# Turning the PSUM banks from block to block, a w_ple product one row block later, and g_final in eight pieces

## The chip, the cores and the metric

The kernel runs on one core of a Trainium2 chip. The metric is the device time of one execution, in microseconds (us), as the median over several runs. The engines are TensorE (PE in the profile, with its weight loads as PEld), VectorE (DVE), ScalarE (ACT), GpSimd (POOL) and SyncE (SP). SP and POOL issue the DMAs.

## The reference

One encoder layer on 256 tokens of width 4096, in float32. Two groups of attention heads (latent attention and dilated window attention) come first; then the output projection, a gated embedding and a last norm. The change touches only what follows the output projection:

```python
x = x + concat([y_a, y_b]) @ w_out                      # (256, 4096)
ple  = p @ w_ple                                        # (256, 256) @ (256, 4096)
gate = sigmoid(rms_norm(x, g_ple) @ w_ple_gate)         # (256, 4096) @ (4096, 4096)
x = x + ple * gate
out = rms_norm(x, g_final)
```

## The kernel before

**A product in three parts.** Every float32 operand of a large product is split in two: `hi` is a copy rounded to a format that PE takes at full speed, made by ACT, and `lo` is the rest, made by DVE (`split`, line 244). `mm` (line 262) then issues three matmuls: hi x hi, hi x lo and lo x hi. Weights come from HBM by DMA into one of four `raw` buffers of 128 x 1024 floats, are split into a pair of tiles, and are used once. A raw buffer is free when DVE has made `lo`, and only then can SP issue the load that uses it next. The pair goes to a ring of three `wp` pairs and, in some stages, a few further buffers.

**Blocks and steps.** The layer is a list of steps, built once and run in order by the loop at the end of `encoder_layer`. A product of 256 x 4096 by 4096 x 1024 is a `Block` (line 1114). A plain step ("c") takes 128 rows of the weights: four products of 128 x 512 (two token tiles by two column halves), 12 matmuls in all. A part of the rows goes through Strassen's scheme of seven products ("f", four steps for each pair of row blocks). The eight sums of a block live in the eight PSUM banks, which have the names m0 to m3, s, o, t0 and t1. `LAST` (line 1504) gives the banks of the three blocks of `w_ple_gate`, in the order M2, X, M3, M4, M1, M5, M6, M7. M2, X, M3 and M4 are open from the first step of a block to its last; M1, M5, M6 and M7 are written by the fast steps only.

**The order in a block.** `spread` (line 1509) lays out six plain steps, 28 fast ones with eight plain ones between them, and four plain ones. For `w_ple_gate` it also puts an "e" into the last four: the product p @ w_ple for the same 1024 columns (`wide_ple`, line 1331), two steps of 12 matmuls, in the banks of M1, M5, M6 and M7. Two tasks empty the banks: `wide_mid` (line 1362) after the last fast step (one ACT copy out of M1, then four DVE additions out of M6, M5, M7 and M5 into the tile `e`, which is `B` in the profile), and `wide_done` (line 1374) after the block's last step (four DVE additions out of M2, X, M3 and M4, then tanh, the product with ple, the addition to x and the squares). After the w_ple product, ACT copies two of its four banks to `Q` and `junk`; the two in t0 and t1 are read in place by `wide_done`.

**Who goes first.** There is no scheduler at run time: each engine has one queue and runs it in the order in which the program was written. The writing is planned. A model of the engines' clocks gives each task a time from which it may go on (`advance`, line 423), and a task is only taken further when `room()` says that splitting the weights has time in hand. `convert_one` (line 1844) writes the splits some steps ahead of their use. So an addition that empties a bank can stand on DVE behind the split of a weight which PE needs only three steps later.

**The end.** Three blocks cover 3072 columns. The other 1024 are done without the fast scheme: two chunks of 512 columns and then 256 and 256 (numbers 6, 7 and 8 in `blocks`), with 32 row blocks each, taken two or four at a time. `tail_banks` (line 1709) names their banks. `g_final` is loaded as a row that is repeated over 128 partitions, in two DMAs of 128 x 2048 on POOL's queue (`load_g`, line 1324), into two buffers (`Al0` and `B5`) that the third block's fast steps read until late; a hook two steps into the tail writes them. `late_gains` (line 1461) multiplies the six finished column chunks by g_final, twelve DVE instructions spread over the tail's steps. `finish` (line 1468) scales each row and stores it.

Nearly all instructions are recorded by one helper, so that they have line 176 in the profile; its groups are told apart by their tiles.

Of the kernel before, what the change touches and what calls it, by code (L numbers as in the profile page):

```python
# [18 lines left out]
P = 128  # L19
# [190 lines left out]
def encoder_layer(ctx: ExitStack, tc: tile.TileContext, x, p, positions, g_mix, w_in, g_q_latent, w_uq,  # L210
# [15 lines left out]
    def slot(tag, shape, dtype=F32):  # L226
        names[tag] = names.get(tag, 0) + 1
        return clock.made(sp.tile([P, *shape], dtype, tag=tag, name=f"{tag}_{names[tag]}"), tag)
# [167 lines left out]
        yield max(flags.at[n] for n in names)  # L396

    begun, due = [-20.0], {}
    lazy = set()
    SOON = 0.3  # L400

    def spawn(task, later=False):
        urgent.append(task)
        due[task] = 0.0
        if later:
            lazy.add(task)

    def resume(pool, task):
        while True:
            clock.stage = 0.0  # L410
            got = next(task, "end")
            due[task] = max(clock.stage, due.get(task, 0.0), got if isinstance(got, float) else 0.0)
            if isinstance(got, Late):
                due[task] += 0.45 if "x dead" in flags else 0.3
            if got == "end":
                pool.remove(task)
                due.pop(task, None)
                lazy.discard(task)
                return
            if not isinstance(got, float) or due[task] > clock.free["pe"] + SOON:  # L420
                return

    def advance(force=False, spare=True):
        if force:
            ahead = [due.get(t, 0.0) for pool in (urgent, running) for t in pool]
            now = clock.free["pe"]
            clock.free["pe"] = max(now, min([d for d in ahead if d > now], default=now))
        now = clock.free["pe"]
        if waiting and len(running) < 5 and now - begun[0] >= waiting[0][2] and waiting[0][0] <= flags:
            needs, task, _ = waiting.pop(0)  # L430
            running.append(task)
            due[task] = max([flags.at[f] for f in needs], default=0.0)
            begun[0] = now
        for pool in (urgent, running):
            for task in list(pool):
                if due.get(task, 0.0) <= clock.free["pe"] + SOON and (force or (spare or task not in lazy) and room() > ROOM):
                    resume(pool, task)


# [659 lines left out]
    class Step:  # L1099
# [5 lines left out]

        def __init__(self, load, split, run, needs=(), frees=0, time=2.73):
            self.load, self.split, self.run, self.needs, self.frees, self.after = load, split, run, needs, frees, None
            self.hold = 0
            self.time = time
            self.ring, self.ring_id = WP, None  # L1110

# [209 lines left out]
        return add_sums(FAST, lambda j: [q[:, 2 * (j % 2):2 * (j % 2) + 2] for q in x1T[j // 2]], z_dst, "B3",  # L1321
                        "x1_sums", x1_s)

    def load_g(i):
        gF.append(slot(("Al0", "B5")[i], [2048]))
        nc.gpsimd.dma_start(gF[i], g_final[2048 * i:2048 * (i + 1)].unsqueeze(0).to_broadcast([P, 2048]))

    P4 = {}
    WIDE_PLE = {(0, 0): "m2", (0, 1): "m3", (1, 0): "t0", (1, 1): "t1"}

    def wide_ple(k):

        ps = {}

        def step(kt):
            box = []

            def load():
                box.append(clock.made(wp.tile([P, 2, Q], F32, tag="raw", name=f"raw_e{kt}", bufs=RAW), "raw", RAW))
                nc.sync.dma_start(box[0].rearrange("p a b -> p (a b)"),  # L1340
                                  w_ple[kt * P:(kt + 1) * P, 1024 * k:1024 * (k + 1)])

            def run(hi, lo):
                for (t, h), tag in WIDE_PLE.items():
                    if kt == 0:
                        ps[t, h] = bank(tag, [Q])
                    mm(ps[t, h], tuple(pT[0][:, i, kt, t * P:(t + 1) * P] for i in range(2)), (hi[:, h], lo[:, h]),
                       kt == 0, kt == 1)
                if kt:
                    spawn(out())  # L1350

            return Step(load, lambda hi, lo: split(hi, lo, box[0]), run, ["pT", ("mid", k)], 1)

        def out():
            for h in range(2):
                nc.scalar.activation(P4[0, h], ps[0, h], AF.Copy)
                P4[1, h] = ps[1, h]
            yield

        return [step(0), step(1)]  # L1360
# [63 lines left out]
    def g_cols(lo, n):  # L1424
        return gF[lo // 2048][:, lo % 2048:lo % 2048 + n]
# [32 lines left out]
                yield from finish(ts[0])  # L1458
        return task

    def late_gains():
        for c in range(2 * WIDE):
            for t in range(NT):
                nc.vector.tensor_tensor(x1[c][:, t], x1[c][:, t], g_cols(512 * c, 512), op=ALU.mult)
                yield
                yield

    def finish(t):
        r, a, h, w = r2[:, t:t + 1], stat(1), stat(1), stat(1)
# [31 lines left out]
        return w[:, lo:lo + n]  # L1501

    hooks = {}
    LAST = "m0", "m1", "s", "o", "m2", "m3", "t0", "t1"

    FAST_COST, PLAIN_COST, PLAIN_TIME = (1.8, 2.3, 1.15, 1.15), 1.15, 2.73
    FAST_TIME = 0.69, 1.37, 1.37, 1.37
# [20 lines left out]
    def lay(blk, order, mid, done, ple=None):  # L1528
        last = max(i for i, o in enumerate(order) if o == "f")
        n = order.count("f") // 4  # L1530
        fast = (x for j in range(n) for x in blk.fast_steps(j))
        rest = list(range(2 * n, 16)) + list(range(16, 32))
        if blk.late:
            rest = rest[16 - 2 * n:] + rest[:16 - 2 * n]
        plain_ = (x for kt in rest for x in blk.plain_step(kt))
        for i, kind in enumerate(order):
            new = {"f": lambda: [next(fast)], "c": lambda: [next(plain_)], "e": lambda: ple}[kind]()
            if i == last:
                new[-1].after = mid
            if i == len(order) - 1:  # L1540
                new[-1].after = done
            for x in new:
                x.ring, x.ring_id = blk.ring, blk
            steps.extend(new)
        return len(steps) - len(order) + last
# [150 lines left out]
                     lambda j: ["pT", ("wide", WIDE - 1)])  # L1696

    for k in range(WIDE):
        order = spread(FAST, 6, 4, (-2,))
        blk = Block(w_ple_gate[:, 1024 * k:1024 * (k + 1)], lhs_x1, x1_s, "x1_sums", order,  # L1700
                    lambda kt: [("x1T", kt // 4)], LAST, "Ah2", WP + ["Al2", "B0"])
        for tag in ("Al2", "B0"):
            allow(blk, tag, lambda i: ran[0] >= out_end - 1)
        blk.fast_needs = [("x1T", c) for c in range(8)]
        blk.turn_needs = [("wide", k - 1)] if k else []
        lay(blk, order, wide_mid(k, blk), wide_done(k, blk), wide_ple(k))
    wide_end = len(steps)
    hook(wide_end + 2, lambda: (load_g(0), load_g(1), spawn(late_gains(), True)))
    tail_banks = {6: (("m2", "m3"), ("t0", "t1")), 7: (("m0", "o"), ("s", "m1")), 8: (("m2", "m3"), ("t0", "t1"))}

    for c, (lo, n) in enumerate(blocks):
        if c < 2 * WIDE:
# [34 lines left out]
    class Old(Step):  # L1747


        def __init__(self, i, ch, j):  # L1750
            self.i, self.ch, self.j, self.ring, self.ring_id = i, ch, j, ch.ring, ch.ring_id
            self.needs, self.after, self.hold = ch.needs(j), None, 0
            self.time = ch.per * len(ch.ts) * 3 * (ch.n / 2370 + 0.011)
            kept_before = ch.keep and not ch.keep[1]
            self.banks = [ch.banks[t] for t in ch.ts] if j == 0 else ()
            self.load = None if kept_before else self.fetch
            self.frees = 0 if kept_before else 1
            self.own = kept_before or ch.keep and j < len(kept)
# [143 lines left out]
    for i, step in enumerate(steps):  # L1902
        if i in hooks:
            for f in hooks[i]:
                f()
        if i < 16 and i % 2 == 0 and 3 + i // 2 < 8:
            next(loads[3 + i // 2])
        lead = i + AHEAD + (3 if len(step.ring) > 3 else max(0, min(3, i - (len(steps) - 25))))
        fetch(lead + 3)
        if i < START:  # L1910
            if 0 < i < 16:
                x_bank((i + 8) % 16)
            if i == 2:
                x_square(8)
            convert(lead + 1)
        n = 0
        while not all(f in flags for f in step.needs) or any(b in locks for b in step.banks) or i not in halves:
            advance(True)
            convert(lead + 1)
            n += 1  # L1920
            assert n < 200, (i, step.needs)
        step_end[0] = clock.free["pe"] + step.time
        step.run(*halves.pop(i))
        ran[0] = i
        if step.after:
            spawn(step.after())
            advance()
        while slack(i) < MARGIN and convert_one(lead + 1):
            pass
        advance(spare=slack(i) > MARGIN)  # L1930
        convert(lead + 1)
# [23 lines left out]
```

## Time and profile before

| | |
|---|---|
| median of 3 runs | 1915.16 us (1914.77 to 1916.81) |
| the profiled execution | 1916.41 us |
| its span in the profile | 1914.6 us |
| PE busy | 1892.6 us, 99% of the span |
| DVE busy | 1636.3 us, 85% |
| ACT busy | 1115.9 us, 58% |
| DMA | 370.61 MB, mean 194 GB/s |

A row of the timeline gives the start in us from the span's start, the duration, the engine, the line, the operation with the tile it writes and those it reads, its shape and how often it was repeated. The brackets at its end hold the idle time of the engine just before it and what ended that time. A row of the chain that ended last gives start, duration and the piece of work, a row of the waits the engine that waited, for whom, the total in us, the number of times and the longest. A row of the DMA issues gives the tiles, the queue, the count, the size of one, and the median time in us from issue to landing, here for the stretch named in the text. Start times are rounded, and the ends of matmuls overlap the next one's start. From one matmul of 512 columns to the next it is 0.2267 us where nothing waits.

### The profile page before, as it was taken

Reading aid. Unit: us, or ns where it says so; the run is one execution under the profiler, and the core shown is the slowest. Engines: PE = TensorE matmul, PEld = TensorE weight load, DVE = VectorE, ACT = ScalarE, POOL = GpSimd, SP = SyncE. Lnnn points to the kernel's source line nnn. Section 1 sums busy time; section 2 is a strip of 40 time slices with the busy share of each in tenths; the row PEclk is TensorE's granted clock in tenths of the full one; section 3 lists DMA queues with packets and bytes.
Section 4 is the critical chain, followed back from the end, with each engine's and each line's share of the span. In section 5 each row is a group of like instructions: output and inputs, shape, how many; then the busy total and the mean of one; then the engine's idle time right before and its main releaser. Section 6 shows DMA issues by size and latency. Waiting matters only on the chain.

```text
span 1914.6 us, 25920 instructions
## 1 busy us (share of the span) xinstructions
PE 1892.6 (99%) x9451; PEld 1614.7 (84%) x9451; DVE 1636.3 (85%) x2276; ACT 1115.9 (58%) x1520; POOL 35.4 (2%) x50
## 2 busy tenths in 40 slices
PE   9999999999999999999999999999999999999997
PEld 6888888888899988888888999888888887888787
DVE  6999999898877789899998777798887988989865
ACT  7655556565577755556565555665554655665543
POOL 1000000000000100000000011000000000000000
PEclk9999999999999999999999999999999999999999
DMA  7566666666654466666667444566666556566665
GB/s 273 183 207 214 215 214 200 196 212 193 186 149 140 142 198 193 192 209 194 214 198 210 136 122 139 170 218 222 206 208 213 171 198 225 181 220 206 203 196 176
DMA packets 159792, 370.61 MB, mean 194 GB/s; under 512 B 28548, under 2 KB 70640, under 8 KB 159408
## 3 DMA queue, kind: packets, MB, share of 16 engines
q1 hardware_dynamic: 158640, 364.97, 60.1%
q0 software_dynamic: 1024, 3.99, 0.6%
q8 instruction: 74, 1.21, 0.3%
q14 instruction: 54, 0.44, 0.1%
HBM read 364.72 MB, written 4.19 MB: 193 GB/s over the span
## 4 chain that ended last, share of the span: by engine, by line
PE 82%; DVE 11%; DMA 3%; issue 2%; ACT 2%; SPq 0%; ACTq 0%; DVEq 0%
PE m L176 48%; PE t L176 15%; PE s L176 10%; PE o L176 9%; DVE lo L176 3%; DVE B L176 3%; DVE T L176 2%; DMA raw<-in_w_ple_gate_dram 2%; DVE Ah L176 1%; DMA raw<-in_w_in_dram 1%; DVE Al L176 1%; ACT hi L176 1%; DVE st L176 0%; ACT T L176 0%; ACT B L176 0%
## 5 line engine op out<-in xcount | busy, mean ns | idle before, releaser
L176 ACT ACTIVATE hi<-raw 128x1024 fp32r<-128x1024 f32 (+3 forms) x455 | 440.9, 977 | 353.7 <-PE t L176 87.1
L176 DVE TENSOR_TENSOR lo<-raw,hi 128x1024 fp32r<-128x1024 f32 (+3 forms) x455 | 505.3, 1120 | 117.2 <-ACT hi L176 114.0
L176 PE MATMUL m<-hi,Ah 128*128 128x512 f32 (+3 forms) x836 | 308.5, 381 | 2.3 <-ACT hi L176 1.8
L176 PE MATMUL m<-hi,Al 128*128 128x512 f32 (+3 forms) x830 | 297.6, 372 | 0.0
L176 PE MATMUL m<-lo,Ah 128*128 128x512 f32 (+3 forms) x713 | 265.9, 373 | 0.7 <-DVE lo L176 0.7
L176 PE MATMUL m<-hi,B 128*128 128x512 f32 (+1 forms) x662 | 205.7, 364 | 1.3 <-DVE B L176 1.3
L176 DVE TENSOR_TENSOR B<-raw,B 128x1024 fp32r<-128x1024 f32 (+2 forms) x201 | 183.7, 926 | 16.5 <-ACT B L176 15.0
L176 PEld LDWEIGHTS m<-hi,Ah 128*128 128x128 f32 x836 | 157.2, 188 | 25.6 <-ACT hi L176 2.5
L176 PEld LDWEIGHTS m<-hi,Al 128*128 128x128 f32 x830 | 155.6, 188 | 22.1
L176 ACT ACTIVATE B<-raw 128x1024 fp32r<-128x1024 f32 (+1 forms) x127 | 117.3, 931 | 90.9 <-DMA raw<-in_w_in_dram 23.6
L176 PEld LDWEIGHTS m<-lo,Ah 128*128 128x128 f32 x713 | 134.2, 188 | 20.8 <-DVE lo L176 3.6
L176 PEld LDWEIGHTS m<-hi,B 128*128 128x128 f32 x662 | 121.3, 189 | 20.4 <-ACT B L176 1.6
L176 PE MATMUL m<-lo,B 128*128 128x512 f32 (+1 forms) x331 | 120.5, 364 | 1.7 <-DVE lo L176 1.6
L176 PE MATMUL m<-B,Ah 128*128 128x512 f32 (+1 forms) x421 | 110.3, 363 | 0.1
L176 DVE TENSOR_TENSOR T<-raw,T 128x512 f32<-128x512 f32 (+2 forms) x107 | 85.2, 808 | 5.0 <-ACT T L176 3.4
L176 PE MATMUL m<-B,Al 128*128 128x512 f32 (+1 forms) x302 | 82.9, 348 | 0.0
L176 PEld LDWEIGHTS m<-B,Ah 128*128 128x128 f32 x421 | 72.3, 189 | 12.4 <-DVE B7b L176 0.5
L176 PE MATMUL t<-hi,Ah 128*128 128x512 f32 (+1 forms) x220 | 81.4, 386 | 0.0
L176 PEld LDWEIGHTS m<-lo,B 128*128 128x128 f32 x331 | 62.6, 189 | 12.4 <-DVE lo L176 3.5
L176 PE MATMUL t<-lo,Ah 128*128 128x512 f32 (+1 forms) x179 | 69.2, 387 | 0.0
L176 PE MATMUL t<-hi,Al 128*128 128x512 f32 x170 | 65.2, 389 | 0.0
L176 DVE TENSOR_TENSOR T<-t,T 128x512 fp32r<-128x512 f32 (+2 forms) x57 | 38.8, 683 | 29.7 <-ACT T L176 29.5
(485 smaller groups left out, 3977.0 us busy)
## 6 DMA issues: line engine op xcount, KB each, us to landing
raw<-in_w_in_dram SPq DMA_DIRECT2D x320, 512.0 KB, 4.3
raw<-in_w_out_dram SPq DMA_DIRECT2D x128, 512.0 KB, 4.5
raw<-in_w_ple_gate_dram SPq DMA_DIRECT2D x128, 512.0 KB, 4.5
raw<-in_w_in_dram SPq DMA_DIRECT2D x48, 384.0 KB, 3.1
raw_q<-in_w_uq_dram SPq DMA_DIRECT2D x32, 256.0 KB, 3.8
raw_k<-in_w_ukv_dram SPq DMA_DIRECT2D x16, 512.0 KB, 3.6
raw<-in_w_in_dram SPq DMA_DIRECT2D x16, 448.0 KB, 3.3
T<-in_x_dram SPq DMA_DIRECT2D x13, 512.0 KB, 6.4
```

Of the source, the lines that this page charges most:

```text
L176: return do(out, *rest, **named)
```

## The change

Four things change.

1. `LAST` and `WIDE_PLE` become lists with one entry for each block. The pairs (m0, m1), (s, o) and (m2, m3) change their roles in turn: block one as before, block two with M2 and X in (m2, m3), M3 and M4 in (m0, m1) and M1 and M5 in (s, o), block three with (s, o), (m2, m3) and (m0, m1). t0 and t1 stay with M6 and M7. The pair that held M1 and M5, and then half of the w_ple product, is the pair in which the next block starts. The tail's banks follow.
2. The "e" goes in at -1 in place of -2: three plain steps stand before the w_ple product and one after it, where it was two and two. SP's loads and the splits change places in the same way.
3. `load_g` issues 128 x 512 pieces on SP's queue, among the loads of weights, eight of them, one every two steps. `late_gains` becomes one task for each column chunk, started five steps after its piece.
4. The task after a block's last fast step is marked `first` and is written at once, whether `room()` has time in hand or not. In the written order this moves two places outside the three blocks: in the second and the third block of the gate projections, the task's ACT copy and its four DVE additions stand ahead of one split that they followed before.

No arithmetic changes, and PE's matmuls are the same in number and size.

```diff
-    def spawn(task, later=False):
+    def spawn(task, later=False, first=False):
         urgent.append(task)
         due[task] = 0.0
         if later:
             lazy.add(task)
+        if first:
+            hot.add(task)
...
-                if due.get(task, 0.0) <= clock.free["pe"] + SOON and (force or (spare or task not in lazy) and room() > ROOM):
+                if due.get(task, 0.0) <= clock.free["pe"] + SOON and (
+                        force or task in hot or (spare or task not in lazy) and room() > ROOM):
                     resume(pool, task)
...
-    def load_g(i):
-        gF.append(slot(("Al0", "B5")[i], [2048]))
-        nc.gpsimd.dma_start(gF[i], g_final[2048 * i:2048 * (i + 1)].unsqueeze(0).to_broadcast([P, 2048]))
+    def load_g(c):
+        if not gF:
+            gF.extend(slot(tag, [2048]) for tag in ("Al0", "B5"))
+        nc.sync.dma_start(g_cols(512 * c, 512), g_final[512 * c:512 * (c + 1)].unsqueeze(0).to_broadcast([P, 512]))
...
-    WIDE_PLE = {(0, 0): "m2", (0, 1): "m3", (1, 0): "t0", (1, 1): "t1"}
+    PAIRS = ("m0", "m1"), ("s", "o"), ("m2", "m3")
+    WIDE_PLE = [dict(zip(((0, 0), (0, 1), (1, 0), (1, 1)), (*PAIRS[2 - k], "t0", "t1"))) for k in range(3)]
...
-    def late_gains():
-        for c in range(2 * WIDE):
-            for t in range(NT):
-                nc.vector.tensor_tensor(x1[c][:, t], x1[c][:, t], g_cols(512 * c, 512), op=ALU.mult)
-                yield
-                yield
+    def late_gain(c):
+        for t in range(NT):
+            nc.vector.tensor_tensor(x1[c][:, t], x1[c][:, t], g_cols(512 * c, 512), op=ALU.mult)
+            yield
+            yield
...
-    LAST = "m0", "m1", "s", "o", "m2", "m3", "t0", "t1"
+    LAST = [(*PAIRS[-k % 3], *PAIRS[(1 - k) % 3], *PAIRS[2 - k], "t0", "t1") for k in range(3)]
...
             if i == last:
-                new[-1].after = mid
+                new[-1].after, new[-1].mid = mid, True
...
-        order = spread(FAST, 6, 4, (-2,))
+        order = spread(FAST, 6, 4, (-1,))
...
-    hook(wide_end + 2, lambda: (load_g(0), load_g(1), spawn(late_gains(), True)))
-    tail_banks = {6: (("m2", "m3"), ("t0", "t1")), 7: (("m0", "o"), ("s", "m1")), 8: (("m2", "m3"), ("t0", "t1"))}
+    for n, c in enumerate((0, 1, 2, 3, 6, 4, 5, 7)):
+        hook(wide_end + 2 + 2 * n, lambda c=c: load_g(c))
+        if c < 2 * WIDE:
+            hook(wide_end + 7 + 2 * n, lambda c=c: spawn(late_gain(c), True))
+    tail_banks = {6: (("m0", "m1"), ("t0", "t1")), 7: (("s", "m3"), ("m2", "o")), 8: (("m0", "m1"), ("t0", "t1"))}
...
         if step.after:
-            spawn(step.after())
+            spawn(step.after(), first=step.mid)
             advance()
```

More of the change, by code (lines that the diff above doesn't have):

```diff
@@ L398, in encoder_layer @@
     begun, due = [-20.0], {}
-    lazy = set()
+    lazy, hot = set(), set()
     SOON = 0.3
-    def spawn(task, later=False):
+    def spawn(task, later=False, first=False):
         urgent.append(task)
@@ L418, in resume @@
                 lazy.discard(task)
+                hot.discard(task)
                 return
@@ L1107, in __init__ @@
             self.load, self.split, self.run, self.needs, self.frees, self.after = load, split, run, needs, frees, None
-            self.hold = 0
+            self.hold, self.mid = 0, False
             self.time = time
@@ L1343, in run @@
             def run(hi, lo):
-                for (t, h), tag in WIDE_PLE.items():
+                for (t, h), tag in WIDE_PLE[k].items():
                     if kt == 0:
@@ L1698, in encoder_layer @@
     for k in range(WIDE):
-        order = spread(FAST, 6, 4, (-2,))
+        order = spread(FAST, 6, 4, (-1,))
         blk = Block(w_ple_gate[:, 1024 * k:1024 * (k + 1)], lhs_x1, x1_s, "x1_sums", order,
-                    lambda kt: [("x1T", kt // 4)], LAST, "Ah2", WP + ["Al2", "B0"])
+                    lambda kt: [("x1T", kt // 4)], LAST[k], "Ah2", WP + ["Al2", "B0"])
         for tag in ("Al2", "B0"):
@@ L1751, in __init__ @@
             self.i, self.ch, self.j, self.ring, self.ring_id = i, ch, j, ch.ring, ch.ring_id
-            self.needs, self.after, self.hold = ch.needs(j), None, 0
+            self.needs, self.after, self.hold, self.mid = ch.needs(j), None, 0, False
             self.time = ch.per * len(ch.ts) * 3 * (ch.n / 2370 + 0.011)
```

## The prediction

> **What bounds the kernel now.** I read the share of busy time first, then the waits of PE in the last 375 us, which hold all the code that the change is about, then the busy time by stretches.
>
> ```profile
> PE 1892.6 (99%) x9451; PEld 1614.7 (84%) x9451; DVE 1636.3 (85%) x2276; ACT 1115.9 (58%) x1520; POOL 35.4 (2%) x50
> ...
> PE m L176 <- DVE B L176: 2.2, 3, 1.3
> PE m L176 <- DVE lo L176: 1.4, 1, 1.4
> ...
> 760.00:1040.00 280.00, 280.00 (x1274) 232.37 (x1273) 254.44 (x301) 167.19 (x183) 0.00 (x0) 1.00 0.65 201
> 1756.00:1786.00 30.00, 29.02 (x129) 23.68 (x127) 26.76 (x32) 16.68 (x19) 1.10 (x2) 1.00 0.71 254
> 1806.00:1852.00 46.00, 46.00 (x204) 38.11 (x203) 30.28 (x34) 22.89 (x29) 0.00 (x0) 1.00 0.55 172
> ```
>
> PE is the bound: busy 99% at a granted clock of 1.00. So an edit can win only what PE waits, and from 1540 us on PE waits four times, 2.2 + 1.4 = 3.6 us by the list. (The columns of the stretches are PE, PEld, DVE, ACT, POOL, clock, share of the DMA engines, GB/s.) The edits cover each of these waits, so each is read in the order of time. A matmul of 128x512 starts 0.2267 us after the one before it, so that a plain step of 12 takes 2.72 us; a wait costs some 0.1 us beside what the list counts, since the first matmul after it is slow.
>
> End of the first block of `w_ple_gate`:
>
> ```profile
> 1616.35 0.69 DVE L176 TENSOR_TENSOR B<-B,m 128x512 f32<-128x512 f32 x1
> 1617.10 0.50 PE L176 MATMUL m<-hi,Ah 128*128 128x512 f32 x1 [0.55 <-DVE B L176]
> 1620.52 0.58 ACT L176 ACTIVATE Q<-m 128x512 f32<-128x512 f32 x1
> 1621.00 0.59 ACT L176 ACTIVATE junk<-m 128x512 f32<-128x512 f32 x1
> 1622.34 1.06 ACT L176 ACTIVATE hi<-raw 128x1024 fp32r<-128x1024 f32 x1 [0.75 <-DMA raw<-in_w_ple_gate_dram]
> 1625.78 1.06 ACT L176 ACTIVATE Al<-raw 128x1024 fp32r<-128x1024 f32 x1 [2.38 <-DMA raw<-in_w_ple_gate_dram]
> 1626.75 0.84 PE L176 MATMUL o<-B,B 128*128 128x512 f32 x3
> 1626.87 1.22 DVE L176 TENSOR_TENSOR Al<-raw,Al 128x1024 fp32r<-128x1024 f32 x1 [2.22 <-ACT Al L176]
> 1628.02 1.28 DVE L176 TENSOR_TENSOR B<-B,m 128x512 f32<-128x512 f32 x2
> 1628.84 0.47 PE L176 MATMUL m<-hi,B 128*128 128x512 f32 x1 [1.26 <-DVE B L176]
> ...
> 1619.34 6.34 DMA raw<-in_w_ple_gate_dram
> ```
>
> First wait: the w_ple product has done its three matmuls into m2 at 1616.38 and wants m3, which DVE's last add of `wide_mid` is still reading; 0.72 us go by, and 0.10 after. Second wait: the block's last matmul ends its turn at 1626.75 + 3 x 0.2267 = 1627.43; the next block starts with m0, whose add stands on DVE behind the split `Al`. That split waits for ACT, ACT for a load that took 6.34 us. The matmul starts at 1628.84: 1.41 us, and 0.08 after.
>
> End of the second block:
>
> ```profile
> 1715.24 1.23 DVE L176 TENSOR_TENSOR lo<-raw,hi 128x1024 fp32r<-128x1024 f32 x1 [1.49 <-ACT hi L176]
> 1716.39 1.28 DVE L176 TENSOR_TENSOR B<-B,m 128x512 f32<-128x512 f32 x2
> 1716.45 0.39 PE L176 MATMUL o<-hi,B 128*128 128x512 f32 x1
> 1717.21 1.62 PE L176 MATMUL m<-Al,B 128*128 128x512 f32 x6 [0.38 <-DVE B L176]
> ```
>
> Third wait: the turn ends at 1716.68, m0's add begins at 1716.39 behind a split, and PE goes on at 1717.21: 0.53 and 0.10. In the third block nothing waits for an eviction, but the `g_final` loads run there, though the code asks for them after it (POOL's queue only waits for the buffers):
>
> ```profile
> 1773.53 0.54 POOL L176 DMA_DIRECT2D B<-in_g_final_dram  x1 [14.39 <-PE t L176]
> 1782.57 0.69 DVE L176 TENSOR_TENSOR Ah<-raw,raw 128x512 f32<-128x512 f32 x1 [2.35 <-DMA raw<-in_w_ple_gate_dram]
> 1782.65 1.06 ACT L176 ACTIVATE hi<-raw 128x1024 fp32r<-128x1024 f32 x1 [4.61 <-DMA raw<-in_w_ple_gate_dram]
> 1785.11 1.22 DVE L176 TENSOR_TENSOR lo<-raw,hi 128x1024 fp32r<-128x1024 f32 x1
> 1786.38 0.50 PE L176 MATMUL m<-lo,B 128*128 128x512 f32 x1 [1.36 <-DVE lo L176]
> ...
> 1773.64 8.90 DMA raw<-in_w_ple_gate_dram
> ...
> Al<-in_g_final_dram POOLq DMA_DIRECT2D x1, 1024.0 KB, 7.9
> B<-in_g_final_dram POOLq DMA_DIRECT2D x1, 1024.0 KB, 9.2
> raw<-in_w_ple_gate_dram SPq DMA_DIRECT2D x13, 512.0 KB, 4.0
> raw<-in_w_ple_gate_dram SPq DMA_DIRECT2D x9, 512.0 KB, 6.1
> ```
>
> Fourth wait: a load of weights issued 0.11 us after the second g load takes 8.90 us. In the stretch 1720 to 1757 such loads land in 4.0 us, from 1757 to 1786, with both g loads in it, in 6.1 (the last two rows). ACT stands 4.61 us, DVE splits late, PE loses 1.52 and 0.10. Together: 0.82 + 1.49 + 0.63 + 1.62 = 4.56 us, the most that these edits can win here.
>
> **The change part by part.**
>
> *w_ple one row block later.* In each block the two w_ple steps and one plain step of 2.72 us trade places; the DMAs trade places on SP likewise, the same bytes. m3 is then wanted at 1619.1, 2 us after its add: the first wait goes, 0.82 us. Blocks two and three have no wait there and win nothing. What gets less room is what follows the product: ACT's two copies (0.58 and 0.59 us) out of its banks have 2.72 us less until the next block. In the changed order they stand behind the split that ran at 1622.34 and ahead of the one at 1625.78. The split ends at 1623.40, so the copies end near 1624.5.
>
> *Rotated banks.* The next block then starts in the two banks that these copies free, and takes the banks of `wide_done`'s adds only with its third product, six matmuls or 1.36 us later. With the first wait gone PE reaches the block at 1626.61, the copies are 2.1 us old, and the first six matmuls run at once. At 1627.97 the third product wants m0. DVE's order around that add is unchanged and hangs on the same load, so the bank comes at 1628.84 again: 0.87 us and 0.08 stay. The boundary and the first wait cost 0.95 in place of 2.31: 1.36 won. At the second boundary the add is wanted at 1716.68 + 1.36 = 1718.04 and comes by 1717.2: 0.63 won. There the copies again stand before a split that PE releases and are done some 3 us ahead. After the third block the tail starts in banks freed by copies in either kernel: nothing. That PE comes 1.36 us sooner into the second block must be met by the splits; DVE stands 1.49 us for a tile that PE has to free (row at 1715.24), so the splits follow PE and have that much in hand.
>
> *g_final in eight pieces.* The third block loses 2 MB of foreign traffic: 1.62 us won, if its loads then land as in the 4.0 us row. The cost is in the tail:
>
> ```profile
> 1820.51 1.06 ACT L176 ACTIVATE hi<-raw 128x1024 fp32r<-128x1024 f32 x1 [1.61 <-PE m L176]
> 1821.60 1.23 DVE L176 TENSOR_TENSOR lo<-raw,hi 128x1024 fp32r<-128x1024 f32 x1 [0.73 <-ACT hi L176]
> 1831.38 1.06 ACT L176 ACTIVATE hi<-raw 128x1024 fp32r<-128x1024 f32 x1 [1.66 <-PE m L176]
> 1863.15 1.23 DVE L176 TENSOR_TENSOR lo<-raw,hi 128x1024 fp32r<-128x1024 f32 x1 [1.88 <-ACT hi L176]
> ...
> raw<-in_w_ple_gate_dram SPq DMA_DIRECT2D x14, 512.0 KB, 4.2
> raw<-in_w_ple_dram SPq DMA_DIRECT2D x1, 256.0 KB, 2.5
> ```
>
> Eight issues go on SP between the loads, one for two steps (5.44 us). They wait for buffers long free, so nothing queues behind them. A piece has 256 KB; a load of that size lands in 2.5 us here. A raw buffer comes free at 1822.83 and its next content is split four splits later, at 1831.38: 8.55 us, of which the load takes 4.2. That leaves 4.3 us, and the split itself, which waits for PE to free one of three tiles, is 5.44 - 2.3 = 3.1 us early. So a piece may delay the load behind it by 7.4 us; I expect 1 to 2.5, and cost it at nothing. The engines' share goes from 0.55 to about 0.55 x (172 + 46) / 172 = 0.70. Without the cover each piece would cost PE up to its 2.5 us, 20 in all. The twelve multiplications by g follow their pieces by at least two weight loads on the same queue; four of them now stand together on DVE (4 x 0.61 = 2.4 us), where DVE stood 1.88 us before the split at 1863.15: 0.55 us late, under one step.
>
> The Trainium skill, page "DMA: Bandwidth & Descriptors", section "Rules for kernel authors", speaks against the cutting: it asks for 1 MiB or more in one DMA, and the fit under "Anatomy of one DMA" (2.0 us and the bytes over 436e3) gives, as an estimate, 8 x 2.6 = 20.8 us for the pieces against 8.8 for two loads, 12 us more if nothing overlaps. The section "Issuing engines are not separate DMA queues" says that loads share the same engines from whichever queue; the landing of 6.1 us beside 4.0 agrees, and by it only the time of the g loads counts, not the queue.
>
> *First turn for the middle evictions.* In two gate blocks it moves one split behind the four adds of `gate_mid`:
>
> ```profile
> 851.16 1.06 ACT L176 ACTIVATE hi<-raw 128x1024 fp32r<-128x1024 f32 x1 [1.68 <-PE t L176]
> 853.40 0.68 DVE L176 TENSOR_TENSOR B<-B,s 128x512 f32<-128x512 f32 x1
> 937.70 0.68 DVE L176 TENSOR_TENSOR B7b<-B7a,t 128x512 f32<-128x512 f32 x1
> ```
>
> The split is some 4 x 0.65 = 2.6 us later. PE is busy 280.00 of 280 us there, and ACT splits only when PE frees one of four tiles, three steps (8.2 us) ahead of use, of which the split takes 2.3. Nothing; without that cover one wait of up to 2.6 us in each block.
>
> Sum: 1.36 + 0.63 + 1.62 = 3.6 us, bounds 2.0 (third-block wait stays) and 4.6. The profiled execution took 1916.41 us (span 1914.6), 1.25 above the median, so a typical run may hold a little less of these waits. I take the sum off the median: 1915.16 - 3.6 = 1911.6.
>
> **The rivals.**
>
> *All of it.* The 0.95 left at the first boundary hangs on one load of 6.34 us; where that lands 0.9 us sooner, nothing is left. For it: such loads have a usual 4 us. Against: four raw buffers are refilled at once there, and the change leaves that. 4.6 us: 1910.6.
>
> *The third block's wait is its own.* Its DVE is busy 26.76 of 30 us, so a split could be late without the g loads. Against: the second block has no such wait. The gain is 2.0 us: 1913.2.
>
> *Slower: the pieces hold up the tail.* Each pair of steps needs 0.55 x 5.44 = 3.0 us of the engines, so a piece may take 2.44 us before loads fall behind. With D us for a piece the tail grows by 8 x (D - 2.44) - 7.4. The 1 MB loads give 9.2 / 4 = 2.3 at the most: against it. For it: the source is one row read 128 times, and 2.5 us is only just above 2.44. The whole gets slower by 3.8 us where D is over 4.3; at 4.5 the time is 1915.16 - 3.6 + 9.1 = 1920.7. The Trainium skill's rule of large DMAs would lead here.
>
> **How the numbers follow.** A change of 0.2%, 3.8 us, is about what a measurement of this kernel can tell from none. Chances: forecast 0.60, all of it 0.20, the third block's wait its own 0.07, slower 0.13. The forecast's own range is 1910.8 to 1912.8 and its middle is 0.2 us short of the bound, 1911.33; I give it half on either side, the better half a little more for the jitter of one load: 0.32 and 0.28. So faster 0.52, same 0.28 + 0.07 = 0.35, slower 0.13. The range 1909.9 to 1914.4 takes in all but the slower case and a small remainder.
>
> **What would show it.** Right: PE's waits from 1540 us on shrink to one of 0.7 to 0.8 us for DVE's `B`, six matmuls into the second block; POOL issues no g load; loads of the third block land in 4 to 5 us; the tail to 1852 us stays at 46.00 of 46. Wrong: PE waits on `lo` or `hi` in the tail, or at the first matmul of a block on ACT (a copy behind a late split), or a wait near 1783 that remains.

## The result

The changed kernel takes 1912.67 us (median of 22 runs, 1911.15 to 1914.97); the kernel before, run beside it, 1916.79 us (22 runs, 1914.74 to 1920.39). The ratio is 0.998, with a 95% interval of 0.9973 to 0.9986: 2.7 to 5.2 us faster, 3.8 us in the middle, against a forecast of 3.6. The time itself is 1.1 us above the forecast of 1911.6, because the median of before is 1.6 us higher over 22 runs than over the three that were known.

The profiled execution took 1913.40 us, with a span of 1911.6: 3.0 us less than the profiled execution of before. First its busy times, its waits of PE from 1540 us on, and three stretches (columns as in the prediction).

```profile
PE 1891.7 (99%) x9451; PEld 1615.2 (84%) x9451; DVE 1635.9 (86%) x2276; ACT 1116.4 (58%) x1520; POOL 35.0 (2%) x48
...
PE m L176 <- DVE lo L176: 0.3, 1, 0.3
...
760.00:1040.00 280.00, 280.00 (x1274) 232.46 (x1273) 254.44 (x301) 167.32 (x183) 0.00 (x0) 1.00 0.67 202
1756.00:1786.00 30.00, 30.00 (x134) 24.83 (x133) 29.76 (x34) 19.49 (x20) 0.00 (x0) 1.00 0.64 209
1806.00:1852.00 46.00, 46.00 (x213) 38.43 (x212) 31.22 (x36) 22.47 (x30) 0.00 (x0) 1.00 0.72 228
```

All four waits are gone: of the 3.6 us in the list of before 0.3 are left, and these are another wait, in the middle of the first block. PE is busy for 30.00 of 30 us in the third block, where it was 29.02. The tail stays at 46.00 of 46 with the pieces in it, and the share of the DMA engines there is 0.72. The gate blocks with the moved split (first row of the stretches) keep their 280.00 of 280.

The four waits were 4.56 us, but the spans differ by 3.0. The rest is lost ahead of the changed code. These are PE's waits up to 1540 us, first of before, then of after:

```profile
PE m L176 <- ACT hi L176: 1.8, 2, 1.1
PE m L176 <- DVE lo L176: 1.6, 6, 0.5
...
```

```profile
PE m L176 <- DVE lo L176: 2.4, 7, 0.8
PE m L176 <- ACT hi L176: 1.6, 2, 0.9
...
PE m L176 <- DVE B7b L176: 0.4, 1, 0.4
...
```

With rows of 1.5, 0.8 and 0.3 that both have and that are left out, PE waits 7.0 us there in place of 6.0. Most of what is added is one wait of 0.8 us for a split of weights near 1284 us; 0.4 us for the tile `B7b` near 186 us come to it. Another 0.55 us goes between 1540 and 1610, ahead of the first moved step. None of these waits stands where the change moved anything, and in the profiles of the experiments they have other sizes: the one near 1284 us is absent from three of them and 0.1 to 0.7 us in the others. So single profiles differ by about what one edit is worth here.

Now the first boundary, where the prediction left 0.95 us. The rows of after:

```profile
1624.58 0.58 ACT L176 ACTIVATE Q<-m 128x512 f32<-128x512 f32 x1
1625.05 0.59 ACT L176 ACTIVATE junk<-m 128x512 f32<-128x512 f32 x1
1626.45 1.06 ACT L176 ACTIVATE Al<-raw 128x1024 fp32r<-128x1024 f32 x1 [0.81 <-DMA raw<-in_w_ple_gate_dram]
1628.12 0.39 PE L176 MATMUL m<-hi,B 128*128 128x512 f32 x1
1628.69 1.28 DVE L176 TENSOR_TENSOR B<-B,m 128x512 f32<-128x512 f32 x2
1629.76 0.40 PE L176 MATMUL m<-lo,B 128*128 128x512 f32 x1
```

The copies stand between the two splits where they were expected, end at 1625.64, and the block starts at 1628.12 without a wait. The addition that frees m0 begins 0.57 us after the block's start, so the third product finds its bank all but free: 0.06 us are lost just ahead of 1629.76. In the prediction the addition began 1.41 us after it (1628.02 against 1626.61).

The pieces, of which each of the first two rows gives the shortest, median and longest time to issue one, in ns, and the first and last start; then the loads of weights in the third block from 1757 to 1786 us, and the loads of the tail from 1806 to 1852 us:

```profile
L176 SPq DMA_DIRECT2D Al<-in_g_final_dram x4: 460/461/462, 1806.6 to 1823.0; - x4
L176 SPq DMA_DIRECT2D B<-in_g_final_dram x4: 460/462/1419, 1828.4 to 1844.7; - x4
...
raw<-in_w_ple_gate_dram SPq DMA_DIRECT2D x9, 512.0 KB, 4.6
...
raw<-in_w_ple_gate_dram SPq DMA_DIRECT2D x15, 512.0 KB, 4.4
B<-in_g_final_dram SPq DMA_DIRECT2D x4, 256.0 KB, 4.5
raw<-in_w_ple_dram SPq DMA_DIRECT2D x1, 256.0 KB, 4.1
```

The third block's loads land in 4.6 us in place of 6.1. In the tail the loads of weights land in 4.4 us, where it was 4.2, and a piece in 4.5.

### The profile page after: what moved, and what is told of

Its sections match the earlier page's. It is cut to its first block, busy times and chain, and to the rows that moved or that the text cites. A ratio compares the mean times of both kernels' runs of the same rounds, so it can differ in the third digit from the quotient of the medians.

```text
span 1911.6 us, 25923 instructions
## 1 busy us (share of the span) xinstructions
PE 1891.7 (99%) x9451; PEld 1615.2 (84%) x9451; DVE 1635.9 (86%) x2276; ACT 1116.4 (58%) x1520; POOL 35.0 (2%) x48
## 4 chain that ended last, share of the span: by engine, by line
PE 85%; DVE 9%; DMA 2%; ACT 2%; issue 2%; SPq 0%; DVEq 0%; ACTq 0%
PE m L176 51%; PE t L176 16%; PE s L176 10%; PE o L176 9%; DVE lo L176 3%; DVE B L176 2%; DVE T L176 2%; DMA raw<-in_w_in_dram 1%; DVE Al L176 1%; DMA raw<-in_w_out_dram 1%; DVE Ah L176 1%; ACT hi L176 1%; DVE st L176 0%; ACT T L176 0%; ACT B L176 0%
## 5 line engine op out<-in xcount | busy, mean ns | idle before, releaser
L176 PE MATMUL m<-hi,Ah 128*128 128x512 f32 (+3 forms) x820 | 302.9, 381 | 1.6 <-ACT hi L176 1.6
L176 PE MATMUL m<-lo,Ah 128*128 128x512 f32 (+2 forms) x705 | 263.1, 373 | 1.0 <-DVE lo L176 1.0
L176 PE MATMUL m<-hi,B 128*128 128x512 f32 (+1 forms) x694 | 215.5, 366 | 0.0
L176 PEld LDWEIGHTS m<-hi,B 128*128 128x128 f32 x694 | 127.3, 189 | 20.3 <-DVE B L176 0.2
L176 PE MATMUL m<-lo,B 128*128 128x512 f32 (+1 forms) x347 | 126.8, 365 | 0.3 <-DVE lo L176 0.3
L176 PE MATMUL m<-B,Al 128*128 128x512 f32 (+1 forms) x323 | 88.1, 351 | 0.0
```

Of the source, the lines that this page charges most:

```text
L176: return do(out, *rest, **named)
```

## The experiments

**One part alone.** Four kernels were run beside each other and beside before (1915.82 us, 33 runs). The first has everything but the pieces: the changed kernel with the old `load_g`, `late_gains` and hook.

```diff
-        nc.sync.dma_start(g_cols(512 * c, 512), g_final[512 * c:512 * (c + 1)].unsqueeze(0).to_broadcast([P, 512]))
+        nc.gpsimd.dma_start(gF[i], g_final[2048 * i:2048 * (i + 1)].unsqueeze(0).to_broadcast([P, 2048]))
...
-    for n, c in enumerate((0, 1, 2, 3, 6, 4, 5, 7)):
-        hook(wide_end + 2 + 2 * n, lambda c=c: load_g(c))
+    hook(wide_end + 2, lambda: (load_g(0), load_g(1), spawn(late_gains(), True)))
```

> The changed kernel with g_final as before: two loads of 1 MB on POOL's queue and one task for the gains. My theory (each wait has one cause; the first three belong to the banks and the w_ple place, the fourth to the g loads): the waits at the ends of the first and second block go, 2.0 to 2.9 us faster than before, and a wait of 1 to 1.7 us on DVE's lo in the third block stays. Rival (the fourth wait is the third block's own and the g pieces win nothing): as fast as the whole change, about 4 us faster than before.

1914.01 us, ratio 0.9988 (0.9979 to 0.9996): 0.8 to 4.0 us faster. Its list of PE's waits from 1540 us on is empty, so the wait that was expected to stay in the third block is not in this profile; more on it below. The second is the opposite: the kernel before with the pieces and their gains alone.

> The kernel before with only the g_final loads and the gains changed (eight pieces on SP among the weights). My theory: the fourth wait goes, 1.6 us faster (1.0 to 2.0), the three waits at the ends of the blocks stay at 2.9 us together, weights of the third block land in 4 to 5 us. Rival (the fourth wait is the third block's own): no gain, and PE still waits over 1 us for a lo some 20 us before the tail.

1916.22 us, ratio 1.0 (0.9991 to 1.0009). The wait in the third block is gone, as expected, but the 1.6 us do not show in the time; the interval runs from 1.7 us faster to 1.7 slower and just leaves room for them. The three boundary waits of before are still there (1.8 us for DVE's `B`); the 0.7 stands in the middle of the first block:

```profile
PE m L176 <- DVE B L176: 1.8, 3, 0.8
PE m L176 <- DVE lo L176: 0.7, 1, 0.7
```

The third moves the w_ple product alone, the fourth turns the banks alone:

```diff
-        order = spread(FAST, 6, 4, (-2,))
+        order = spread(FAST, 6, 4, (-1,))
```

> The kernel before with only the w_ple product one row block later. My theory (both waits of the first boundary hang on the one DVE chain behind a late load): the first wait, 0.82 us, goes, and the second grows by as much, because the next block starts in m0, whose add comes when it came before: no gain (0.3 us either way). Rival (the parts add up, each wait goes by itself): 0.8 us faster.

1917.09 us, ratio 1.0004 (0.9995 to 1.0013).

```diff
-    WIDE_PLE = {(0, 0): "m2", (0, 1): "m3", (1, 0): "t0", (1, 1): "t1"}
+    PAIRS = ("m0", "m1"), ("s", "o"), ("m2", "m3")
+    WIDE_PLE = [dict(zip(((0, 0), (0, 1), (1, 0), (1, 1)), (*PAIRS[2 - k], "t0", "t1"))) for k in range(3)]
...
-    LAST = "m0", "m1", "s", "o", "m2", "m3", "t0", "t1"
+    LAST = [(*PAIRS[-k % 3], *PAIRS[(1 - k) % 3], *PAIRS[2 - k], "t0", "t1") for k in range(3)]
```

> The kernel before with only the banks rotated (w_ple where it was, g_final and the middle evictions as before). My theory: the wait for m3 ahead of the w_ple product stays (0.8 us), the two waits at the starts of the second and third block go, 1.4 + 0.6 = 2.0 us faster, as much as banks and place together where the load is as late as in the profile. Rival (the parts add up): 2.1 us here and 2.9 with the place; or, if the two ACT copies now come too late, the start of a block waits for ACT and the gain is under 1 us.

1914.84 us, ratio 0.9994 (0.9985 to 1.0003). The waits of PE from 1540 us on, first of the moved product alone, then of the turned banks alone (the rows of 1.4 and 1.0 for DVE's `lo` are the wait in the third block):

```profile
PE m L176 <- DVE B L176: 2.1, 2, 1.7
PE m L176 <- DVE lo L176: 1.4, 1, 1.4
...
1629.38 0.47 PE L176 MATMUL m<-hi,B 128*128 128x512 f32 x1 [1.72 <-DVE B L176]
```

```profile
PE s L176 <- DVE lo L176: 1.0, 1, 1.0
PE m L176 <- DVE B L176: 0.2, 1, 0.2
```

Moving the product alone wins nothing, and the trace shows why: the wait of 0.82 us at 1617 is gone, and PE comes to the next block's start earlier and waits there for the same chain on DVE, 1.88 us in place of 1.41. Turning the banks alone takes away the waits at the two block starts and keeps that at 1617 (0.36 us in this run, where 0.8 was expected). So the moved product needs the turned banks; the banks alone clear two of the three waits, and only both together clear all three, but for up to 0.30 us that is counted below. No interval of these parts but the first excludes zero; that the waits go is shown by the traces, how many microseconds each part carries is not settled by the times. The middle values, 2.3 us without the pieces (0.9988) and nothing for the pieces alone, leave 1.5 of the 3.8 us unassigned, and the intervals are wide enough for either part to carry them.

**The term of 0.95 us.** The chain that the prediction took as fixed can be read in several profiles. First the rows of the moved product alone, then those of everything but the pieces:

```profile
1626.32 1.06 ACT L176 ACTIVATE Al<-raw 128x1024 fp32r<-128x1024 f32 x1 [1.49 <-PE m L176]
1628.55 1.28 DVE L176 TENSOR_TENSOR B<-B,m 128x512 f32<-128x512 f32 x2
```

```profile
1624.54 1.06 ACT L176 ACTIVATE Al<-raw 128x1024 fp32r<-128x1024 f32 x1 [1.04 <-DMA raw<-in_w_ple_gate_dram]
1625.98 0.39 PE L176 MATMUL m<-hi,B 128*128 128x512 f32 x1
1626.78 1.28 DVE L176 TENSOR_TENSOR B<-B,m 128x512 f32<-128x512 f32 x2
```

From the start of ACT's copy for the split `Al` to the addition it is 2.23 us and 2.24 here, 2.24 in before and 2.24 in after: the order on DVE does hold the addition behind that split, as the prediction had it. What varies is when the copy starts, and in three of these four profiles it is a load of weights that sets it. Counted from PE's arrival at the block, the addition begins 1.41 us late by the prediction's working from before, 1.05 in the moved product alone (1628.55 against 1629.38 less the 1.88), 0.80 with everything but the pieces and 0.57 in after. The bank has to come 1.36 us after the arrival and comes 0.82 us after the addition's start (1628.84 less 1628.02), so that up to 0.54 us cost nothing. The 0.80 should cost 0.26; 0.29 us are measured. In the eight profiles that have both edits (after and seven experiments) the wait at this place, with the slow matmuls after it, is 0 three times, 0.06 to 0.09 three times, and 0.29 and 0.30.

**The mark for the first turn.** The changed kernel without it:

```diff
-            spawn(step.after(), first=step.mid)
+            spawn(step.after())
```

> The changed kernel without the first turn for the middle evictions; banks, place and pieces stay. Theory (the first turn does nothing: ACT and DVE have room where it moves a split): the changed kernel's time, 0.2% below before, within 1 us. Rival (it carries a part: banks, place and first turn together won 0.12%, banks alone 0.06% and place alone lost 0.04%, so that 0.10% or 1.9 us are not in the two): 1.9 us slower than the changed kernel, 0.1% below before.

1913.25 us, beside 1916.34 of before; ratio 0.9981 (0.9972 to 0.999), where the changed kernel has 0.998. The mark carries nothing that can be measured.

**Where the fourth wait comes from.** Banks, place and mark with the two old g loads, each issued twice:

```diff
-        nc.gpsimd.dma_start(gF[i], g_final[2048 * i:2048 * (i + 1)].unsqueeze(0).to_broadcast([P, 2048]))
+        for _ in range(2):
+            nc.gpsimd.dma_start(gF[i], g_final[2048 * i:2048 * (i + 1)].unsqueeze(0).to_broadcast([P, 2048]))
```

> Banks, place and first turn of the changed kernel with g_final as before (two loads of 1 MB on POOL, which run in the third block), each of the two loaded twice: 4 MB of foreign traffic in the third block in place of 2. Theory (the fourth wait comes from these loads): the weights' loads land in 6 us and more from 1757 to 1795 and PE waits there for DVE's lo or ACT's hi, 1.5 to 6 us in all; the time is as much longer than with the single loads, 0.1 to 0.3%. Rival (the wait was the third block's own): no more waits there than with the single loads, the same time.

1914.11 us, ratio 0.9985 (0.9975 to 0.9994): as fast as with single loads, and the wait is 0.75 us (0.58 in the list), under the 1.5 expected. The trace shows why twice the bytes are not twice the pressure: POOL issues the second copy of a load only when the first has landed, so that, but for 0.8 us after 1773.46, there is one g load at a time beside the weights.

```profile
1758.51 0.56 POOL L176 DMA_DIRECT2D Al<-in_g_final_dram  x1 [269.29 <-PE t L176]
1766.45 0.54 POOL L176 DMA_DIRECT2D Al<-in_g_final_dram  x1 [7.37 <-DMA Al<-in_g_final_dram]
1773.46 0.53 POOL L176 DMA_DIRECT2D B<-in_g_final_dram  x1 [6.47 <-PE t L176]
1783.73 0.53 POOL L176 DMA_DIRECT2D B<-in_g_final_dram  x1 [9.73 <-DMA B<-in_g_final_dram]
...
1773.41 8.28 DMA raw<-in_w_ple_gate_dram
1785.54 0.50 PE L176 MATMUL s<-lo,B 128*128 128x512 f32 x1 [0.58 <-DVE lo L176]
```

The last two rows are the load that SP issues beside the second g load, from the chain that ended last, and the matmul that waits. The same pair of rows with turned banks alone; then the load with the moved product alone; then, with everything but the pieces, POOL's issue of the second g load and the split that such a load of weights releases:

```profile
1771.08 8.79 DMA raw<-in_w_ple_gate_dram
1783.71 0.50 PE L176 MATMUL s<-lo,B 128*128 128x512 f32 x1 [0.98 <-DVE lo L176]
```

```profile
1774.25 8.94 DMA raw<-in_w_ple_gate_dram
```

```profile
1770.24 0.54 POOL L176 DMA_DIRECT2D B<-in_g_final_dram  x1 [14.39 <-PE t L176]
1777.55 1.06 ACT L176 ACTIVATE hi<-raw 128x1024 fp32r<-128x1024 f32 x1 [2.81 <-DMA raw<-in_w_ple_gate_dram]
```

So the wait of PE rises with the landing of one load: 8.94 us and 1.61 with the moved product alone, 8.90 and 1.52 in before, 8.79 and 1.14 with turned banks alone, 8.28 and 0.75 with the loads doubled. There is none with everything but the pieces, where that load was issued at 1769.82, 0.42 us ahead of the g load, and landed in 7.6 us; the split that it releases starts 7.31 us after POOL's issue (1777.55 less 1770.24; 9.12 in before). That last profile is of the fastest of its kernel's runs, 1911.53 us against a median of 1914.01, so its missing wait is no proof against the g loads. Each of these pairs is one execution.

**Cut, queue and time of the g loads.** Two loads of 1 MB on the weights' queue in the tail, and the eight pieces on POOL's queue, which runs ahead into the third block. Both against the changed kernel:

```diff
+        if n in (0, 4):
+            hook(wide_end + 2 + 2 * n, lambda i=n // 4: load_g(i))
```

> The changed kernel with g_final in two loads of 1 MB on the weights' queue, asked for where the first and the fifth of the eight pieces stood: same queue, same place, same bytes, not cut. Theory (what counts is that the bytes no longer fall into the third block; the tail has room): the changed kernel's time within 1 us, the third block without a wait; a load behind a 1 MB load lands in 6 to 9 us as it did beside such loads on POOL, and the cover found with three and five copies (about 4 us over the 4.2 us of a load) just holds. Rival (the cutting is what makes the tail cheap): the loads of weights behind each 1 MB load come late, 1 to 3 us of waits for DVE's lo after 1806 and after 1828. Other rival, the Trainium skill's rule of large loads (page DMA: Bandwidth & Descriptors): faster than with eight pieces; no more than the 0.6 us of waits left in the tail is there to be won.

```diff
-        nc.sync.dma_start(g_cols(512 * c, 512), g_final[512 * c:512 * (c + 1)].unsqueeze(0).to_broadcast([P, 512]))
+        nc.gpsimd.dma_start(g_cols(512 * c, 512), g_final[512 * c:512 * (c + 1)].unsqueeze(0).to_broadcast([P, 512]))
```

> The changed kernel with the eight pieces on POOL's queue, which runs ahead of the code: the bytes fall into the third block again, as in the kernel before, though cut. Theory (the fourth wait is one load of weights that lands in over 7.5 us because it is issued just behind a g load: 8.9 us and 1.5 us of wait in before, 8.8 and 1.1 with banks alone, 8.3 and 0.75 with the loads doubled, about 7.1 and no wait with banks, place and first turn): pieces of 256 KB that POOL issues four at once act like the 1 MB load, so that PE waits 0 to 1.6 us near 1783 for DVE's lo; the time 0 to 1.6 us above the changed kernel's. Rival (queue and size matter, not when): no wait in the third block, the changed kernel's time, loads there in 4 to 5 us.

1913.11 us, ratio 0.9983 (0.9974 to 0.9992), and 1913.19 us, 0.9981 (0.9972 to 0.999), beside 1916.56 of before. Neither differs from the changed kernel. The g loads of each, the two late ones first:

```profile
Al<-in_g_final_dram SPq DMA_DIRECT2D x1, 1024.0 KB, 6.1
B<-in_g_final_dram SPq DMA_DIRECT2D x1, 1024.0 KB, 6.8
```

```profile
Al<-in_g_final_dram POOLq DMA_DIRECT2D x4, 256.0 KB, 7.2
B<-in_g_final_dram POOLq DMA_DIRECT2D x4, 256.0 KB, 6.5
...
1756.00:1786.00 30.00, 30.00 (x134) 24.84 (x133) 29.65 (x34) 19.33 (x20) 4.29 (x8) 1.00 0.81 278
```

Neither the cut nor the queue makes a difference that these runs can tell. With the pieces back in the third block PE still does not wait there in that profile; the load of weights that was issued beside the late pieces landed in 5.9 us. So the times do not show that the bytes had to leave the third block: cut and early they cost nothing that can be measured, whole and early 0.9988 (0.9979 to 0.9996) stands against 0.9981, and the intervals overlap. With the two late loads the weights of the tail land in 4.4 us in the median, not in the 6 to 9 expected, and PE waits nowhere in the tail. The Trainium skill's rule of 1 MiB or more (page "DMA: Bandwidth & Descriptors", section "Rules for kernel authors") favours the two loads; by the estimate in the prediction they would be 12 us ahead if nothing overlapped. The page gives the fit behind that estimate for loads that GpSimd issues, while the pieces and the two late loads go out on SP. The runs show no difference, and in the tail of both kernels PE has no wait in the list.

**How much room the tail has.** Every piece three times, and five times; the copies go to buffers that nobody reads.

```diff
+        for i in range(2):
+            nc.sync.dma_start(spare[2 * pieces[0] + i], g_final[512 * c:512 * (c + 1)].unsqueeze(0).to_broadcast([P, 512]))
```

> The changed kernel with every piece of g_final loaded three times (two copies go to buffers that nobody reads): 24 DMAs of 256 KB in place of 8 in the tail. Theory (pieces are hidden by the cover that the prediction worked out): in the changed kernel the share of the DMA engines in 1806 to 1852 rose from 0.55 to 0.72, so a piece takes 0.17 x 46 / 8 = 0.98 us of all engines. A pair of steps then needs 3.0 + 3 x 0.98 = 5.9 us of 5.44: 0.5 us too much, 8 times, 3.9 us in all, below the cover of 7.4. The time stays at the changed kernel's, within 1 us; the share comes near 1. Rival (a piece holds the loads up for 2.44 us or more, and one for a pair is just what fits): 3.0 + 3 x 2.44 = 10.3 us for 5.44; 8 x 4.9 - 7.4 = 32 us slower.

> The changed kernel with every piece loaded five times: 40 DMAs of 256 KB in the tail. Theory: 3.0 + 5 x 0.98 = 7.9 us of the engines for a pair of steps of 5.44; 8 x 2.45 = 19.6 us too much, less the cover of 7.4: about 12 us slower than the changed kernel, with PE waiting in the tail for DVE's lo and ACT's hi behind late loads. If the cover were not there, 20 us. Rival (a piece costs only its issue on SP, 0.46 us): 5 x 0.46 = 2.3 us for a pair, beside loads that SP issues in 0.33 us each; no change.

1916.92 us, ratio 1.0 (0.9991 to 1.0009), and 1939.32 us, 1.0121 (1.0105 to 1.0137). Against the changed kernel that is some 4 us and 26 us slower, where 0 and 12 were expected. The stretch from 1806 to 1852 us and its loads, with three and with five copies:

```profile
1806.00:1852.00 46.00, 44.69 (x197) 36.08 (x197) 27.27 (x30) 20.57 (x27) 0.00 (x0) 1.00 0.98 283
...
raw<-in_w_ple_gate_dram SPq DMA_DIRECT2D x14, 512.0 KB, 9.5
...
1857.68 0.38 PE L176 MATMUL s<-hi,B7a 128*128 128x256 f32 x1 [0.43 <-ACT hi L176]
1858.94 0.39 PE L176 MATMUL s<-lo,B7a 128*128 128x256 f32 x1 [0.88 <-DVE lo L176]
```

```profile
1806.00:1852.00 46.00, 38.20 (x148) 29.14 (x146) 20.37 (x24) 16.60 (x23) 0.00 (x0) 0.93 0.96 239
1826.00:1836.00 10.00, 6.89 (x23) 4.91 (x22) 2.96 (x3) 2.11 (x2) 0.00 (x0) 0.79 1.01 247
...
1831.86 0.80 PE L176 MATMUL m<-hi,B 128*128 128x512 f32 x1 [2.65 <-ACT hi L176]
```

A plain count of bytes, at the rate that each run itself shows, agrees in size: before moved 172 GB/s in these 46 us, 7.9 MB; 24 pieces of 0.262 MB make 14.2 MB, and at the 283 GB/s of the first row 50.2 us, 4.2 too many (4 measured). With 40 pieces it is 18.4 MB; at 239 GB/s 77 us, 31 too many (26 measured, and a part of these is the slower clock of the second fence). So no cover of 7.4 us is to be seen. The engines are full, but SP also stands 15.0 us with three copies, between 1800 and 1900 us, until earlier loads have landed, and not at all in after; whether the bytes alone or this queueing too sets the 4 us was not separated. Of the waits with three copies, 2.5 us in all, 1.3 stand in the last two rows of the first fence, in the steps of 256 columns just behind the stretch.

## Why the prediction was right

The reasons hold, but one term of the sum was mis-sized and the size of another is not confirmed, both because they were read from one profile. Of the signs that were named for "right", three came: POOL issues no g load, the third block's loads land in 4.6 us, the tail stays at 46.00 of 46. The first did not: one wait of 0.7 to 0.8 us for DVE's `B` was to remain, and none is in the list.

- *w_ple later*: right. The wait of 0.82 us is gone. The place alone moves it to the block's start, as its working has it, though 0.47 us of it and not all.
- *Turned banks, second boundary*: right, 0.63 us gone.
- *Turned banks, first boundary*: the mechanism was right and a size was off. The 0.87 us and 0.08 that should stay, 0.95 in all, measured 0.06 in after and at most 0.30 in the eight profiles. The step took the bank's arrival at 1628.84 as fixed; it hangs on a load, and that of before was the latest of the profiles shown. The rival "all of it" had this right, for the reason that it gave.
- *The g loads*: the 1.62 us went, and the rows speak for the cause (one load of weights that lands late beside a g load). But the wait is a matter of each execution, 0 to 1.61 us in the profiles with a g load there, and the pieces alone show no gain (1.0, 0.9991 to 1.0009), which leaves them at most 1.7 us on the kernel before. How much they carry on average stays open.
- *Nothing lost in the tail*: right for these pieces, and so the rival "slower" fell. The share of 0.70 was 0.72. A piece lands in 4.5 us, not 2.5, and the load behind it hardly later (4.4 in place of 4.2). But the cover of 7.4 us was worked out too wide: three copies should have cost nothing and cost 4 us. As far as the runs show, the formula was wrong twice: it added the split's own lead to the room of one load, and the working with three copies scaled the engines' share, which at 0.98 moves less for each part (289 GB/s for a whole against 317 at 0.72). Which of the two took the cover away was not tested.
- *First turn for the middle evictions*: right, nothing.
- *The third block's wait its own*: fell. There is no such wait in any of the six profiles without a g load in the third block, and in four of the six with one there is.

The sum of the four waits was 4.56, the forecast 3.6, the measured middle 3.8 with 2.7 to 5.2 around it: the forecast and "all of it" can't be told apart by the times, only by the rows. That 3.6 and 3.8 lie so close is in part luck: the first boundary gave more than its term, and what the g loads gave on average is not known. In the working of the chances the middle of the range from 1910.8 to 1912.8 is 0.5 us short of 1911.33, not 0.2; this touches the chances alone.

## What to carry to other kernels

Where several waits stand one behind another on the same chain, an edit that removes the first only feeds the second; look for the edit further along the chain that must go with it. A wait that hangs on one load has no fixed size: read the landing of that load in more than one profile before it becomes a term of a sum. Whether a few transfers are cut, or on which queue they go, did not matter here while the DMA engines had room; count bytes over the stretch before trusting a cover.

## What was not expected of the hardware

- Full DMA engines (share 0.96 to 0.98) moved 239 to 283 GB/s in the tail. At a share of 0.72 they moved 228, which scaled to a whole would be 317: the rate of a part-filled stretch can't be scaled up. Nor is 283 a ceiling for other loads: with the g loads doubled, the third block from 1756 to 1786 us moved 294 GB/s at a share of 0.85.
- With five copies the granted clock fell to 0.79 from 1826 to 1836 us, around one wait of PE of 2.65 us; the matmul after it took 0.80 us, where the first one after a wait takes 0.47 to 0.50 in the rows of the other kernels (rows of five copies above). So late loads cost PE twice. The Trainium skill, page "TensorE: Matmul & The Clock Gate", section "HAM oscillation — how this bites in real kernels", gives the rule that gaps over about 3.4 us bring the clock down; here the clock fell at a gap of 2.65 us, and the measurement decides.
- A broadcast piece of 256 KB landed in 4.5 us where a load of weights of 256 KB had landed in 2.5. That is not the broadcast: the same load of weights landed in 4.1 us in after, and in 6.7 with three copies. The landing goes with what else is under way.
